# Leaving a streaming kernel with one barrier instead of two, with GpSimd awaiting the last store

## The chip, the cores and the metric

The kernel runs on one core of a Trainium2 chip. The metric is device time in microseconds (us) of one execution, lower being better. Nanoseconds are written ns.

A few words that recur. An engine is one of the core's five units with its own instruction stream: TensorE, VectorE (DVE in the profile), ScalarE (ACT), GpSimd (POOL) and SyncE (SP, which issues the transfers here). They synchronise by semaphores. Drains and events are instructions of an engine's instruction stream that wait for semaphores or add to them; the exit is built of them. The span is the time from the first to the last instruction of the kernel in a trace. The landing is the last update of the last store's semaphore.

## The reference, cut to what matters

```python
def setup_inputs():
    return {"x": np.random.randn(64, 256, 8192).astype(np.float32)}

def reference(x):
    return np.mean(x, axis=2)
```

Half a gigabyte is read, 64 KB are written.

## The kernel before

All loads are issued by SyncE, in 63 blocks of 256 rows and one last block in small pieces. VectorE sums along rows, with a little help from ScalarE. TensorE transposes the sums of the 63 blocks for one store; the last block goes out in two stores of half a kilobyte. The very last store is this:

```python
    def store_last(r):
        nc.vector.transpose(out=fin_t[r][:], in_=fin[r][:])
        return nc.sync.dma_start(out=out_last[r], in_=fin_t[r][0:P:SQ, :])
    ...
    untracked(scaled_sum(fin[1][:, 0:1], fin_in[:, 0 : lastw + k]))._wait_ge(sem, 16)
    with tc.issue_after(st.ins):
        store_last(1)
    ctx.close()
    tc.close()
    tc.compile()
```

What matters here stands in no line of the source: closing the tile context adds an exit block. In the built program it reads as follows (each engine runs its own lines in this order; G is the gather semaphore of the barrier, R its release semaphore):

```
SyncE    3 event waits and a drain: the 3 stores, and the last work of the 4 other engines
ScalarE, TensorE, VectorE, SyncE   drain: when R is 0, add 1 to G
ScalarE, TensorE, VectorE, SyncE   event: when R is 1 or more, take 1 from R
GpSimd   drain; event (gather): when G is 4, take 4 from G; event (release): add 4 to R
GpSimd   drain (reset); clear of the kernel's semaphores 99 to 118
the four engines and GpSimd        a second barrier, the same as the first
```

## Time and profile before

| | before |
|---|---|
| median of the timed runs | 1246.84 us (1246.76 to 1246.90, 3 runs) |
| span of the profiled execution | 1245.24 us |
| last transpose ends | 1242.76 us |
| last store issued | 1242.79 us |
| landing | 1244.35 us |
| landing to end of span | 898 ns |

The times from "last store issued" on are single records of the trace: starts of instructions, and updates of semaphores. No view prints the updates; they were read from the trace file itself, here and below. This is how to read the exit as a view. Each row is one engine, with q for its sequencer (PEldq is TensorE's), and one operation at the line of the exit; then the count, the shortest, middle and longest duration in ns, and the start of the first and the last, in us. Before:

```profile
L172 SPq EVENT_SEMAPHORE  x5: 17/28/28, 1243.4 to 1245.2; - x5
L172 POOLq EVENT_SEMAPHORE  x4: 17/17/17, 1244.5 to 1245.1; - x4
L172 POOLq DRAIN  x3: 34/89/389, 1.1 to 1245.0; - x3
L172 SPq DRAIN  x3: 7/7/13, 1244.4 to 1244.7; - x3
...
L172 PEldq EVENT_SEMAPHORE  x2: 51/51/51, 1244.7 to 1245.2; - x2
```

SyncE has five events (three waits, two releases) and GpSimd four (two gathers, two releases). TensorE's event, the longest at 51 ns, is there twice: once for each barrier. The second ends the span.

### The profile page before, as it was taken

What the parts mean: (1) busy time and instruction counts of PE and PEld (TensorE: products, weight loads), DVE (VectorE), ACT (ScalarE), POOL (GpSimd) and SP (SyncE); (2) the same over time, 40 slices, a digit from 0 to 9 for tenths busy, and PEclk for the clock granted to TensorE, in tenths of its full rate; (3) what the DMA queues carried; (4) which work ended last, traced back from release to release, by engine and by line L of the source; (5) the groups of instructions that cost most, each with busy time, mean ns of one, the idle gap of its engine ahead of it and who ended that gap; (6) DMA issues with size and microseconds to landing.
All of it is one profiled execution on the core that took longest, in us unless ns stands there. A gap on an engine that the chain in (4) does not pass through costs nothing.

```text
span 1245.2 us, 227 instructions
## 1 busy us (share of the span) xinstructions
PE 0.9 (0%) x2; PEld 0.4 (0%) x2; DVE 1087.4 (87%) x79; ACT 16.5 (1%) x13; POOL 0.7 (0%) x6
## 2 busy tenths in 40 slices
PE   0000000000000000000000000000000000000000
PEld 0000000000000000000000000000000000000000
DVE  3898988989889889898898988989889898898898
ACT  0000000000000000000000000000000000000004
POOL 0000000000000000000000000000000000000000
DMA  9999999999999999999999999999999999999998
GB/s 438 417 425 438 438 438 438 434 408 438 438 438 438 438 438 432 411 438 438 438 438 438 438 415 427 438 438 438 438 438 436 406 438 438 438 438 438 438 429 348
DMA packets 10169, 536.95 MB, mean 431 GB/s; under 512 B 1145, under 2 KB 1464, under 8 KB 1720
## 3 DMA queue, kind: packets, MB, share of 16 engines
q1 hardware_dynamic: 10168, 536.94, 99.8%
q14 instruction: 1, 0.01, 0.0%
HBM read 536.87 MB, written 0.07 MB: 431 GB/s over the span
## 4 chain that ended last, share of the span: by engine, by line
DMA 70%; DVE 29%; SPq 0%; issue 0%; DVEq 0%
DMA xt<-in_x_dram 70%; DVE res L92 29%; DVE fin_in L92 0%; SPq L82 0%; DVE fin_in L98 0%; DVE fin_t L109 0%; DVEq L98 0%
## 5 line engine op out<-in xcount | busy, mean ns | idle before, releaser
L92 DVE TENSOR_REDUCE res<-xt 128x2 f32<-128x16384 f32 (+1 forms) x63 | 1076.4, 17086 | 153.3 <-DMA xt<-in_x_dram 153.3
L95 ACT ACT_TABLE_LOAD x1 | 1.3, 1283 | 1181.3 <-DVE res L92 1181.3
L95 ACT ACTIVATE xt<-xt 128x8192 f32<-128x8192 f32 (+5 forms) x6 | 14.7, 2443 | 43.9 <-DMA xt<-in_x_dram 43.7
L92 DVE TENSOR_REDUCE fin_in<-xt 128x1 f32<-128x256 f32 (+3 forms) x5 | 5.0, 1005 | 0.3 <-DMA xt<-in_x_dram 0.2
L92 DVE TENSOR_REDUCE head<-xt 128x1 f32<-128x4096 f32 x1 | 4.4, 4420 | 0.2 <-DMA xt<-in_x_dram 0.2
L153 PE MATMUL ps<-ident,res 128*63 128x128 f32 x2 | 0.9, 460 | 1230.4 <-ACT xt L95 1229.3
L95 ACT ACTIVATION_READ_ACCUMULATOR xt<-xt 128x1 f32 x6 | 1.1, 186 | 0.0
L72 DVE MEMSET fin<- 128x32 f32 x2 | 0.1, 85 | 0.9 <-PEq L230 0.9
L154 DVE TENSOR_SCALAR bulk<-ps 63x128 f32<-63x128 f32 x2 | 0.6, 278 | 0.4 <-PE ps L153 0.4
L153 PEld LDWEIGHTS ps<-ident,res 128*63 128x63 f32 x2 | 0.4, 180 | 1230.6 <-issue 1229.2
L98 DVE TENSOR_SCALAR_CACHE_REDUCE fin_in<-fin_in 128x265 f32<-128x265 f32 x1 | 0.4, 431 | 0.2 <-DVE fin_in L92 0.2
L109 DVE STREAM_TRANSPOSE fin_t<-fin 128x32 f32<-128x32 f32 x2 | 0.4, 212 | 0.1
L60 POOL TENSOR_SCALAR_AFFINE_SELECT ident<-ident 128x128 f32<-128x128 f32 x1 | 0.3, 295 | 0.1
L98 DVE TENSOR_SCALAR_CACHE_REDUCE head<-head 128x2 f32<-128x2 f32 x1 | 0.2, 156 | 0.1
L59 POOL MEMSET ident<- 128x128 f32 x1 | 0.2, 205 | 0.4 <-POOLq L230 0.4
L230 POOL MEMSET const-bfloat16-1.0<- 128x1 bf16 x1 | 0.1, 103 | 0.0
L230 POOL MEMSET const-uint8-127<- 128x1 uint8 x1 | 0.1, 103 | 0.0
L230 POOL MEMSET const-float32-0.0<- 128x1 f32 x1 | 0.1, 99 | 0.2 <-issue 0.2
L230 POOL MEMSET const-float32-1.0<- 128x1 f32 x1 | 0.1, 99 | 0.0
L98 DVE DVE_READ_ACCUMULATOR head<-head 128x1 f32 x1 | 0.1, 85 | 0.0
L98 DVE DVE_READ_ACCUMULATOR fin_in<-fin_in 128x1 f32 x1 | 0.1, 84 | 0.0
## 6 DMA issues: line engine op xcount, KB each, us to landing
xt<-in_x_dram SPq DMA_DIRECT2D x1, 4096.0 KB, 31.2
xt<-in_x_dram SPq DMA_DIRECT2D x1, 2048.0 KB, 35.7
xt<-in_x_dram SPq DMA_DIRECT2D x1, 1024.0 KB, 37.7
xt<-in_x_dram SPq DMA_DIRECT2D x63, 40.8
xt<-in_x_dram SPq DMA_DIRECT2D x1, 512.0 KB, 38.5
xt<-in_x_dram SPq DMA_DIRECT2D x1, 256.0 KB, 38.7
xt<-in_x_dram SPq DMA_DIRECT2D x1, 128.0 KB, 38.6
fin_in<-in_x_dram SPq DMA_DIRECT2D x1, 128.0 KB, 38.4
```

Of the source, the lines that this page charges most:

```text
L59: nc.gpsimd.memset(ident[:], 0.0)
L60: nc.gpsimd.affine_select(out=ident[:], in_=ident[:], compare_op=mybir.AluOpType.not_equal, fill=1.0, base=0, pattern=[[-1, P]], channel_m ...
L72: nc.vector.memset(fin[r][:], 0.0)
L92: return untracked(nc.vector.tensor_reduce(out=dst, in_=src, axis=X, op=ADD))
L95: return untracked(nc.scalar.activation(out=src, in_=src, func=COPY, accum_out=dst))
L98: return nc.vector.tensor_scalar(out=src, in0=src, scalar1=inv, scalar2=None, op0=mybir.AluOpType.mult, op1=ADD, accum_out=dst,)
L109: nc.vector.transpose(out=fin_t[r][:], in_=fin[r][:])
L153: nc.tensor.transpose(out=ps[:LB, :], in_=res[:, r, :], identity=ident[:])
L154: nc.vector.tensor_scalar_mul(out=bulk[:LB, :, r], in0=ps[:LB, :], scalar1=inv)
L230: nc = _bacc.Bacc("TRN2", target_bir_lowering=False, num_devices=1)
```

## The change

The exit keeps one barrier. SyncE no longer awaits the last store. GpSimd's gather does, beside the four arrivals. Then GpSimd clears the semaphores, and only then releases the others. The second barrier, SyncE's own drain and GpSimd's drains around the clear go away.

```diff
-        store_last(1)
+        last_store = store_last(1)
...
+    exit_ins = list(end_bb.instructions)
+    waiter, waits = exit_ins[0], exit_ins[0].sync_info.on_wait
+    stored = last_store.ins.sync_info.on_update[0].id
+    drain, gather, release, _, clear = [
+        i for i in exit_ins if i.engine == mybir.EngineType.Pool
+    ][:5]
+    with nc.body("awaits", parent=parent, valid_engines=[mybir.EngineType.SP]):
+        for w in waits:
+            if w.id != stored:
+                nc.sync.wait_ge(bass.SemaphoreHandle(w.ant_name, w.id), w.wait_value)
+    bass.BassInstruction(gather)._wait_ge(
+        bass.SemaphoreHandle(last_store.ins.sync_info.on_update[0].ant_name, stored), 16
+    )
...
+    end_bb.instructions = [
+        *awaits.instructions, *exit_ins[1 : exit_ins.index(drain)], drain, gather, clear, release
+    ]
```

(Two asserts and the lines that take the helper block out of the list are cut.)

More of the change, by code (lines that the diff above doesn't have):

```diff
@@ L215 @@
     head_bb.instructions.insert(at, hint)
+    exit_ins = list(end_bb.instructions)
+    waiter, waits = exit_ins[0], exit_ins[0].sync_info.on_wait
+    assert waiter.engine == mybir.EngineType.SP and isinstance(waiter, mybir.InstDrain)
+    stored = last_store.ins.sync_info.on_update[0].id
+    drain, gather, release, _, clear = [
+        i for i in exit_ins if i.engine == mybir.EngineType.Pool
+    ][:5]
+    assert isinstance(clear, mybir.InstISA)
+    with nc.body("awaits", parent=parent, valid_engines=[mybir.EngineType.SP]):
[5 more added lines that the diff above has]
+    )
+    awaits = next(b for b in blocks if b.name == "awaits")
+    blocks.remove(awaits)
+    end_bb.instructions = [
+        *awaits.instructions, *exit_ins[1 : exit_ins.index(drain)], drain, gather, clear, release
+    ]
 _INS = ['x']
```

## The prediction

> **What bounds the kernel now.** I read the page from the top, then the chain of work that ended last, then the waits of SyncE, then the instructions of the exit, and at last the single records of the final 3 us. The page's head, its slices and its chain say what the 1245 us are made of:
>
> ```profile
> span 1245.2 us, 227 instructions
> PE 0.9 (0%) x2; PEld 0.4 (0%) x2; DVE 1087.4 (87%) x79; ACT 16.5 (1%) x13; POOL 0.7 (0%) x6
> DMA  9999999999999999999999999999999999999998
> HBM read 536.87 MB, written 0.07 MB: 431 GB/s over the span
> DMA xt<-in_x_dram 70%; DVE res L92 29%; DVE fin_in L92 0%; SPq L82 0%; DVE fin_in L98 0%; DVE fin_t L109 0%; DVEq L98 0%
> ```
>
> The 16 DMA engines are at 90% or more in every slice but the last. The kernel streams 536.87 MB; VectorE, busy for 87%, keeps step behind it. The bound of the whole is the load. Nothing in this change touches a load or a sum, so at most the last few microseconds can move. The chain, in order of time, shows where the work stops:
>
> ```profile
> 1240.44 1.49 DVE fin_in L92 x3
> ...
> 1242.07 0.45 DVE fin_in L98 x2
> 1242.52 0.02 issue
> 1242.55 0.21 DVE fin_t L109
> ```
>
> The last computing instruction, the transpose, ends at 1242.76 us; the span ends at 1245.24. So 2.48 us at the end are store and exit. The waits of SyncE from 1242 to 1246 us (who waited for whom; us in total, times, longest) split them:
>
> ```profile
> SPq L110 <- DVE fin_t L109: 1.2, 1, 1.2
> SPq L172 <- DMA out_dram<-fin_t: 0.9, 1, 0.9
> SPq L172 <- PEq L172: 0.6, 2, 0.5
> ```
>
> The second line is SyncE waiting for the last store to land. The third is its two waits for the release in two barriers; the engine named is only whoever touched the release semaphore, the release itself comes from GpSimd. The instructions on the exit's line from 1244.69 us on (durations in ns) show that barrier number two is nearly empty of work:
>
> ```profile
> L172 POOLq DRAIN  x1: 89/89/89, 1244.7 to 1244.7; - x1
> ...
> L172 POOLq EVENT_SEMAPHORE_RANGE_CLEAR  x1: 142/142/142, 1244.8 to 1244.8; - x1
> ```
>
> **The exit, record by record.** Starts in us, from the trace: last store issued by SyncE 1242.786 (511 ns of issue); the last update of its semaphore 1244.346; SyncE's event wait for it starts 1244.363, its plain drain 1244.428, its barrier drain 1244.498; that one's update arrives 1244.506. GpSimd's gather starts 1244.530, its release 1244.608, update 1244.633. Then GpSimd alone: drain 1244.694, clear of the semaphores 1244.813, drain 1244.983, second gather 1245.062, second release 1245.140, update 1245.165. TensorE leaves last: its event starts 1245.193 and takes 51 ns, to 1245.244, which is the end of the span.
>
> **What the Trainium skill says.** "Perfetto Trace Analysis", section "Sequencer-only Instruction (DRAIN, etc)": the profiler reports only the execution, not the wait before it nor the spread of the semaphore update after it. The trace agrees: GpSimd's gather is recorded with 17 ns, but from its start to the next instruction's start are 78 ns, and its update is seen 25 ns after its start. So I add starts, not durations. "DMA: Bandwidth & Descriptors", section "Anatomy of one DMA — SWDGE (gpsimd) path": of a fixed cost of about 2 us most is the receipt of the write, and the semaphore can't fire before it. Here issue to landing is 1244.346 - 1242.786 = 1.56 us for 0.5 KB, issued by SyncE rather than GpSimd; the same kind, somewhat shorter, and nothing that a barrier can shorten. "Runtime: NRT & Kernel Launch", section "The ~15µs preamble/postamble breakdown": after the kernel the runtime runs its own barrier over all engines. The trace shows it: updates of a semaphore that is not the kernel's run from 1245.523 to 1246.003 and again to 1247.149.
>
> **The change part by part.** It takes away SyncE's wait for the last store with the drain behind it, GpSimd's three drains but the first, the whole second barrier (a drain and an event wait on each of four engines, a gather and a release on GpSimd). It adds one condition to GpSimd's gather: the last store's semaphore at 16. In the built program this is one instruction with two waits and its decrement, not two instructions. It moves the clear between gather and release. The loads, sums and stores are the same on all engines, in the same order.
>
> SyncE's other waits are done well before: its first event wait starts at 1243.368 and successive ones are about 70 ns apart, so with three waits and the barrier drain it arrives near 1243.61, 0.7 us before the store lands. The other three engines have arrived by then: the updates of the gather semaphore by ScalarE and VectorE are at 1241.673 and 1242.818, TensorE's earlier. So the store stays the last thing waited for.
>
> From the landing at 1244.346 to the end, before:
> - landing to the release of barrier one: 1244.633 - 1244.346 = 287 ns;
> - release one to release two: 1245.165 - 1244.633 = 532 ns;
> - release two to TensorE's end: 1245.244 - 1245.165 = 79 ns. Sum 898 ns.
>
> After:
> - landing to GpSimd's gather: 24 ns (as 1244.506 to 1244.530);
> - gather to clear: 78 ns (gather to release before, start to start), or 89 as an event with two waits is recorded with 28 rather than 17 ns on SyncE;
> - clear to release: 170 ns (clear to drain before, start to start); up to 33 more if the pause before an event after the clear is the 61 ns seen between two events and not the 28 ns seen before the drain;
> - release to update 25 ns; update to TensorE's end 79 ns.
> Sum 376 to 420 ns. Removed: 898 - 420 = 478 to 898 - 376 = 522 ns; I take 500.
>
> All of this is on the path, none of it beside other work: after the landing nothing else runs. Span after: 1245.24 - 0.50 = 1244.74 us. The timed runs stand 1246.84 - 1245.24 = 1.60 us above the span (the profiled execution itself read 1247.03). I keep that as a constant, since every engine is let go by the same release event as before: 1244.74 + 1.60 = 1246.34 us, 0.04% less.
>
> **The rivals.**
> (a) The runtime's barrier swallows part. Its first eight updates are 35, 160, 44, 23, 99, 39, 34 and 46 ns apart (differences of the records); at the start of the execution the same walk has 34, 39, 44, 23, 113, 38, 34 and 47. The second step is thus some 120 ns late: one engine comes late to it. If what delays that engine does not hang on the kernel's release, up to 0.12 us of the gain is lost (1246.46), in the worst case all (1246.84). Against it: all engines come from the same release, so their lateness should move along.
> (b) Instruction fetches. The exit gets shorter by 2 to 4 instructions on each engine, so what follows lies elsewhere. "Runtime: NRT & Kernel Launch", section "Instruction fetch mechanics", says that a taken branch out of the present window forces a fetch before execution goes on. The trace has one 8192-byte instruction transfer near the end, at 1242.604, 43 ns after VectorE's branch, of 455 ns; it is over at 1243.06, long before the release, so it is hidden. If a fetch came onto the path it would cost some 0.5 us at least (estimate from that transfer) and eat the gain: 1246.8 to 1247.3. Fewer instructions make an added fetch unlikely.
> (c) A wait takes the place of the one removed: GpSimd wakes more slowly from the store's semaphore than SyncE (17 ns), or the clear right behind a wait costs more than behind a drain. Every such step costs tens of ns: 0.1 us, 1246.45.
> (d) Nothing to be seen: the three runs lie within 0.14 us, but another load of the program may shift 1246 us of streaming by more than 0.5 us; the transfers' slices range from 406 to 438 GB/s. This moves the result both ways.
>
> **Range and chances.** (a) to (c) lean upwards by 0 to 0.5 us, (d) adds about 0.5 us either way. I take 1245.5 to 1247.1. Two per cent are 25 us; the whole stretch after the last computation is 2.5 us, so neither side is in reach: 0.995 for within 2%, the rest for a disturbance of the chip.
>
> **What would show it right or wrong.** Right: in SyncE's waits at the exit the line for the store is gone and the release wait occurs once, about 0.9 us long or more; one clear, GpSimd with two event instructions at the exit instead of four and one drain; landing to end of span near 0.40 us against 0.90; store issue to landing still about 1.56 us; span about 0.5 us less as far as the last transpose ends at the same time. Wrong in a step: clear or release starts more than 50 ns off the sums above (c), an instruction transfer after 1243 us (b), the runtime's updates not closer behind the kernel's end as before (a), or the last transpose moving by more than the gain (d).

## The result

| | before | after |
|---|---|---|
| median of the same rounds | 1246.87 us (1246.76 to 1247.29, 6 runs) | 1246.30 us (1246.10 to 1246.69, 6 runs) |
| mean of the same rounds | 1246.91 us | 1246.37 us |
| span of the profiled execution | 1245.24 us | 1244.90 us |
| landing to end of span | 898 ns | 367 ns |

The ratio is 0.9996, with a 95% interval of 0.9983 to 1.0009: the same, by the 2% measure. A ratio here is the mean time of one kernel's fast runs over that of the other's of the same rounds, so not quite the ratio of the medians. The output is correct.

The page's head and the end of the chain of work, after:

```profile
span 1244.9 us, 214 instructions
...
HBM read 536.87 MB, written 0.07 MB: 431 GB/s over the span
```

```profile
1242.26 0.45 DVE fin_in L98 x2
1242.70 0.02 issue
1242.73 0.21 DVE fin_t L109
```

The stream is as before: the same bytes at the same rate. In this execution the last transpose even started 0.18 us later (1242.73 against 1242.55), which is why the two spans differ by 0.35 us only. From the transpose's end at 1242.94 to the end of the span the kernel takes 1244.90 - 1242.94 = 1.96 us, against 2.48. SyncE's waits near the end, after:

```profile
SPq L110 <- DVE fin_t L109: 1.2, 1, 1.2
SPq L172 <- PEq L172: 0.9, 1, 0.9
```

SyncE's wait for the store is gone. In its place it waits once, 0.9 us, for the only release. The time of the store did not vanish: another engine waits for it. The exit after:

```profile
L172 POOLq EVENT_SEMAPHORE  x2: 17/272/526, 1244.0 to 1244.8; - x2
L172 POOLq DRAIN  x1: 386/386/386, 1.1 to 1.1; - x1
...
L172 SPq DRAIN  x1: 253/253/253, 1243.8 to 1243.8; - x1
L172 POOLq EVENT_SEMAPHORE_RANGE_CLEAR  x1: 139/139/139, 1244.6 to 1244.6; - x1
...
L172 PEldq EVENT_SEMAPHORE  x1: 51/51/51, 1244.8 to 1244.8; - x1
```

GpSimd has two events instead of four. One of them, the gather, is recorded with 526 ns: its record opens when the four arrivals are there (1244.032) and closes after the store has landed (1244.558), so part of the wait shows as duration. TensorE has one event. In single records, counted from the landing, with the end of the last instruction of GpSimd and of the span:

| ns after the landing | before | after |
|---|---|---|
| GpSimd's gather starts / ends | 184 / 201 | before the landing / 30 |
| first release starts | 262 | none |
| clear starts | 467 | 94 |
| last release starts | 794 | 263 |
| GpSimd's last instruction ends | 811 | 280 |
| TensorE's last instruction ends: end of span | 898 | 367 |

So 531 ns went from the exit. The store itself took the same from issue to landing (1.560 and 1.562 us).

### The profile page after: what moved, and what is told of

Same layout as the page of the kernel before. It is cut to its first block, busy times and chain, and to the rows that moved or that the text cites. A ratio compares the mean times of both kernels' runs of the same rounds, so it can differ in the third digit from the quotient of the medians.

```text
span 1244.9 us, 214 instructions
## 1 busy us (share of the span) xinstructions
PE 0.9 (0%) x2; PEld 0.4 (0%) x2; DVE 1087.4 (87%) x79; ACT 16.5 (1%) x13; POOL 0.7 (0%) x6
## 4 chain that ended last, share of the span: by engine, by line
DMA 70%; DVE 29%; SPq 0%; issue 0%; DVEq 0%
DMA xt<-in_x_dram 70%; DVE res L92 29%; DVE fin_in L92 0%; SPq L82 0%; DVE fin_in L98 0%; DVE fin_t L109 0%; DVEq L98 0%
```

## The experiments

The totals of the full kernels scatter by some tenths of a microsecond. So most experiments use a short kernel: cut to 4 of its 64 blocks, it keeps the exit word for word and has a sixteenth of the stream. Such a kernel leaves most of the output unwritten, and its result is wrong. Its edit is one line:

```diff
-    N = B * C
+    N = 4 * 256
```

**The two kernels, cut.**

> The kernel before, cut to the first 4 of the 64 blocks of rows (the rest of the output is not written, so the result is wrong on purpose), so that the streaming and its scatter shrink by 16 while the exit stays word for word. All theories: last landing of the store to end of span 0.90 us as in the long kernel, store issue to landing about 1.56 us. Total near 85 us (536.87 MB take 1240 us, so 33.6 MB take 78, and some 8 for start and end), scatter of the runs below 0.2 us.

> The changed kernel, cut likewise. Main theory (the gain is the exit, all of it on the path): landing to end of span 0.37 us, and the timed total is 0.53 us below short_before. Rival 1 (the 0.57 us between the long medians are partly scatter of the streaming, or the runtime's closing barrier swallows a part): the records of the exit shrink by 0.53 but the total falls by 0.4 or less. Rival 2 (something earlier also became faster): the total falls by more than 0.6.

Measured: 85.59 us in the median before (85.48 to 85.80, 5 runs) and 85.17 after (85.04 to 85.27, 5 runs). The means are 85.61 and 85.15, so 0.46 us apart. From landing to end of span 893 and 368 ns, issue to landing 1.552 and 1.555 us. The exit is the one of the long kernel, to 5 ns in its length. The scatter of the short kernel before is 0.32 us rather than the 0.2 expected, so the scatter does not come from the stream alone. The difference of 0.46 lies between main theory and rival 1, so these totals alone don't decide; the records of the closing walk (the runtime's own barrier after the kernel, below) do.

**Only the wait moved.** Both barriers stay; GpSimd's first gather awaits the store. SyncE's own drain, which held one of its waits, goes away too.

```diff
-    end_bb.instructions = [
-        *awaits.instructions, *exit_ins[1 : exit_ins.index(drain)], drain, gather, clear, release
-    ]
+    end_bb.instructions = [*awaits.instructions, *exit_ins[1:]]
```

> One part alone: GpSimd's first gather awaits the last store, SyncE awaits the rest, both barriers and the drains stay. Main theory: landing to the first release's start falls from 262 to 94 ns (as measured in the changed kernel up to its clear), the rest stays, so 0.73 us from landing to end and 0.17 us less than short_before in total. Rival (nearly all comes from the barrier taken away, the hop over SyncE lies beside other work): less than 0.05 us.

Measured: 85.51 us in the median (85.33 to 85.66), mean 85.48, so 0.13 below the short kernel before. These runs overlap with that kernel's, so the records must decide. Landing to first release 92 ns, landing to end 729 ns: 164 less than the 893. The hop over SyncE lay on the path. The exit's view of this kernel:

```profile
L172 POOLq EVENT_SEMAPHORE  x4: 17/17/514, 82.6 to 83.7; - x4
...
L172 PEldq EVENT_SEMAPHORE  x2: 51/51/51, 83.2 to 83.7; - x2
```

Four GpSimd events and two of TensorE say that both barriers are there; the 514 ns show the gather that holds the store's wait.

**Only one barrier.** SyncE awaits the store as before.

```diff
-    with nc.body("awaits", parent=parent, valid_engines=[mybir.EngineType.SP]):
-    ... (the wait moved to GpSimd)
     end_bb.instructions = [
-        *awaits.instructions, *exit_ins[1 : exit_ins.index(drain)], drain, gather, clear, release
+        *exit_ins[: exit_ins.index(drain)], drain, gather, clear, release
     ]
```

> The other part alone: one barrier with the clear between gather and release, while SyncE awaits the store as before. Main theory: landing to GpSimd's gather 184 ns as before, 78 to the clear, 170 to the release, 104 to the end: 0.54 us, so 0.36 us less than short_before. If the parts add up, this and the moved wait make 0.53 together. Rival as for the moved wait: 0.5 us or more from this part alone.

Measured: 85.26 us (85.10 to 85.38), mean 85.25, so 0.37 below the mean of the short kernel before. Landing to end 532 ns, 361 less. The parts add up: 164 + 361 = 525 ns, and both together measured 893 - 368 = 525. The view shows SyncE awaiting the store, and one barrier:

```profile
SPq L172 <- DMA out_dram<-fin_t: 0.9, 1, 0.9
SPq L172 <- PEq L172: 0.3, 1, 0.3
```

**Where the time goes after the kernel's end.** The timed runs stand about 1.8 us above their spans in both kernels (1246.69 against 1244.9 in the profiled execution after). In the trace, after the kernel's last instruction, one semaphore of the runtime is updated nine times, then again nine times. The first series is taken here as a closing walk that the engines take part in one after the other; the kernels without a release, below, bear this out. In the changed kernel its steps come 606, 640, 852, 896, 919, 1017, 1056, 1090 and 1137 ns after the landing. The third comes 212 ns after the second, where most are 23 to 47 ns apart: some engine is late there. The next experiments ask which, and whether it hides part of the gain.

> The changed kernel once more, at full size, in more rounds. Main theory: 0.51 us below the kernel before (0.53 in the exit, 0.01 given back in the runtime's closing walk). If the 0.57 us between the first medians were partly scatter, the difference of the means lies elsewhere, but between 0.3 and 0.7.

Measured: 1246.18 us in the median (1245.95 to 1246.92, 5 runs) against 1246.69 (1246.50 to 1246.94, 9 runs) for the kernel before on that chip. The means are 1246.29 and 1246.69, 0.40 us apart. From landing to end of span 367 ns again, and the same nine steps to within 1 ns.

**No release at all.** The other engines add to the gather and leave; GpSimd clears and leaves.

```diff
-    end_bb.instructions = [
-        *awaits.instructions, *exit_ins[1 : exit_ins.index(drain)], drain, gather, clear, release
+    leave = [
+        i
+        for i in exit_ins[1 : exit_ins.index(drain)]
+        if not isinstance(i, mybir.InstEventSemaphore)
     ]
+    assert len(leave) == 4
+    end_bb.instructions = [*awaits.instructions, *leave, drain, gather, clear]
```

> The changed kernel, full size, without the release: the other engines add to the gather and leave, GpSimd clears and leaves; the runtime's own closing walk over the engines is then what joins them. The kernel's end is then the end of the clear, 94 + 139 = 233 ns after the landing, against 367: span 0.13 us less. What the total does tells which engine holds up the closing walk. If GpSimd is the engine that comes late to its third step (about 565 ns after GpSimd's last instruction in both kernels), it only starts some 47 ns sooner and the total falls by 0.05 us. If it is one of the engines that wait for the release, the total falls by 0.13 to 0.24 us.

> The same cut to 4 of 64 blocks (wrong result on purpose), beside short_after with 85.15 us in the mean: landing to end of span 0.23 us. Last update of the closing walk counted from the landing: 1.14 us in the changed kernel; 1.08 if GpSimd is the late engine, 0.9 to 1.0 if not.

Measured: at full size 1246.40 us (1245.96 to 1246.76), mean 1246.37, which is not below the 1246.29 of the changed kernel on that chip. Cut, 85.11 us (84.99 to 85.92), mean 85.24 with the one run at 85.92. The span falls as expected, 233 ns from landing to end, but the totals show no gain that stands out of the scatter. The trace tells why. The first step of the walk now comes 12.8 us before the landing, shortly after TensorE's exit, and the second 2.5 us before it, 159 ns after ScalarE's. The third comes 771 ns after the landing, 538 after GpSimd's last instruction, and the walk ends at 1056 instead of 1137 (cut: 770 and 1056). GpSimd is the third step, and its way there is long in itself. The walk gained 81 ns, more than the 47 expected; 37 of them are lost again between the two series, which no run explains. The last update of the second series is at 2238 instead of 2282 ns: 44 ns gained. That is near the 0.05 us expected, in part by luck.

```profile
L172 POOLq EVENT_SEMAPHORE  x1: 519/519/519, 1243.4 to 1243.4; - x1
L172 POOLq EVENT_SEMAPHORE_RANGE_CLEAR  x1: 139/139/139, 1243.9 to 1243.9; - x1
```

These are the last two rows of the exit: no engine has a release event any more, and the clear is the kernel's last instruction.

**Release first, clear last.**

```diff
-        *awaits.instructions, *exit_ins[1 : exit_ins.index(drain)], drain, gather, clear, release
+        *awaits.instructions, *exit_ins[1 : exit_ins.index(drain)], drain, gather, release, clear
```

> The changed kernel, cut likewise, with the release ahead of the clear, so the clear lies beside the others' leaving. The other engines leave 169 ns sooner (release 94 ns after the landing), GpSimd ends about 94 + 78 + 139 = 311 ns after the landing instead of 280. If GpSimd is the engine that the closing walk waits for, the total is the same or 0.03 us more than short_after; if one of the released engines is, it falls by 0.1 us or more.

Measured: 85.21 us (84.96 to 85.26), mean 85.15, the mean of the short changed kernel on another chip. GpSimd's last instruction ends 312 ns after the landing. The other four leave 171 ns sooner, and the first two steps of the walk move with them, from 606 and 640 to 435 and 469. The third does not: 849 against 852. It follows GpSimd alone.

Here is what all traces say together, in ns after the landing:

| kernel | GpSimd's last instruction ends | third step | walk ends | second series ends |
|---|---|---|---|---|
| before, full | 811 | 1372 | 1657 | 2803 |
| short before | 805 | 1366 | 1652 | 2796 |
| short, wait moved only | 640 | 1202 | 1487 | 2630 |
| short, one barrier only | 444 | 1016 | 1301 | 2446 |
| after, full | 280 | 852 | 1137 | 2282 |
| short, clear last | 312 | 849 | 1135 | 2278 |
| no release, full | 233 | 771 | 1056 | 2238 |

The third step comes 537 to 572 ns after GpSimd's last instruction in every row. It is 537 or 538 where the clear is GpSimd's last instruction, and 561 to 572 where a release event is. So the gain that reaches the outside follows GpSimd's own end, within 25 ns in these rows: for the change itself 811 - 280 = 531 became 2803 - 2282 = 521 ns.

**SyncE takes the exit over.** If GpSimd is slow on the way to the walk, it should not be the last to leave. Here there is no barrier of the kernel's own: SyncE awaits by their semaphores the last units of the others and the three stores, then clears. The engines are joined by the runtime's walk alone.

```diff
-    bass.BassInstruction(gather)._wait_ge(
-        bass.SemaphoreHandle(last_store.ins.sync_info.on_update[0].ant_name, stored), 16
-    )
+        nc.sync.wait_ge(
+            bass.SemaphoreHandle(last_store.ins.sync_info.on_update[0].ant_name, stored), 16
+        )
+        nc.sync.sem_clear(range(99, 119))
...
-    end_bb.instructions = [
-        *awaits.instructions, *exit_ins[1 : exit_ins.index(drain)], drain, gather, clear, release
-    ]
+    end_bb.instructions = [*awaits.instructions]
```

> Full size, no barrier of the kernel's own at the end: SyncE awaits the last units of the four other engines and the three stores by their semaphores, the last store last, then clears the range itself; the others leave as soon as their work is done. Only the runtime's closing walk joins them. From the earlier runs GpSimd is the third step of that walk and takes 538 to 572 ns from its last instruction to it, while the step that the released engines answer for comes about 240 to 285 ns after their last instruction. If the 540 ns belong to GpSimd and SyncE is among the quick ones (the fifth, turning step), the first walk ends some 0.7 to 0.8 us after the landing against 1.14 in the changed kernel, and the total falls by 0.3 to 0.4 us below the changed kernel. Rival: the 540 ns belong to whichever engine leaves last; then the walk ends at about 1.05 us and the total falls by 0.1 us or less.

> The changed kernel again at full size, on the same chip as sp_exit, to compare with it: 0.5 us below the kernel before, within a scatter of the means of about 0.15 us; from the landing to the span's end 0.367 us and to the end of the first walk 1.137 us as in its two traces so far.

> The same exit by SyncE in the kernel cut to 4 of 64 blocks (wrong result on purpose), where the scatter of the totals is about 0.1 us: 0.3 to 0.4 us below short_after_again if GpSimd's way to the walk is slow in itself, 0.1 or less if it is the last engine's whoever that is. Landing to end of the kernel's span about 0.23 us either way.

> The changed kernel, cut to 4 of 64 blocks, again, on the chip of short_sp_exit: 85.15 us in the mean as before, give or take 0.1; landing to end of span 0.368 us.

Measured, all on one chip:

| | median | mean |
|---|---|---|
| before, full | 1246.81 us (1246.60 to 1247.14, 9 runs) | 1246.83 |
| after, full | 1246.17 us (1246.11 to 1246.79, 5 runs) | 1246.35 |
| exit by SyncE, full | 1245.59 us (1245.28 to 1245.85, 5 runs) | 1245.58 |
| after, cut | 85.10 us (85.07 to 85.21, 5 runs) | 85.12 |
| exit by SyncE, cut | 84.46 us (84.33 to 84.82, 5 runs) | 84.55 |

The full version is correct in these runs; that its engines may leave one by one rests on the runtime's walk, which joins them. It is 0.77 us below the changed kernel in the mean and 1.25 below the kernel before; cut, 0.57 below the changed kernel. None of its runs overlaps one of the other two. By the 2% measure it is the same too (0.9989, interval 0.9976 to 1.0003). I had expected 0.3 to 0.4 us; two things are cheaper than thought. The exit's two last rows of SyncE, each from the view of its own line, are:

```profile
L232 SPq EVENT_SEMAPHORE  x1: 28/28/28, 1244.3 to 1244.3; - x1
```

```profile
L235 SPq EVENT_SEMAPHORE_RANGE_CLEAR  x1: 61/61/61, 1244.4 to 1244.4; - x1
```

The same clear of 20 semaphores takes 61 ns on SyncE against 139 on GpSimd, so the span ends 142 ns after the landing. And SyncE is in the walk 126 ns later, at 268 ns, as its fifth and turning step; the four others had taken theirs before the landing. The walk ends at 432 ns against 1137, and the second series at 1618 against 2282 (cut: 426 and 1616): 0.66 us by the records, between the 0.57 and 0.77 of the totals. The rival, by which the 540 ns belong to whichever engine leaves last, falls.

## Why the prediction was right

**The bound and the reach.** Right. The stream did not change, nothing but the exit moved, and the result is within 2%. The forecast was 1246.34 us, measured were 1246.30.

**The sum of the exit.** Right in mechanism and nearly in size: 478 to 522 ns were worked out for the removed part, 531 were measured. After the landing 376 to 420 ns were expected, and 367 came. The mis-sized term is the step from landing to clear: 24 ns to the gather and 78 to 89 from there, 102 to 113 in all, against 94 measured. The gather does not start afresh at the landing; it is already open and ends 30 ns after it. Clear to release measured 169 against 170 (the extra 33 for a pause did not come), release to end 104 as worked out.

**What lies beside other work.** The prediction had SyncE at the barrier near 1243.61, 0.7 us before the landing. Its arrival came at 1244.007, in an execution that ran 0.18 us late throughout, so about 0.22 us later than worked out. The reason is the barrier drain: 253 ns in place of the 7 ns that it took behind a landed store. It cost nothing, as the landing came 0.52 us later still. The prediction took the duration of a drain from a place behind a landed store; here it stood behind a store just issued. What the drain waits for is not shown.

**The constant of 1.60 us.** Wrong as a number, harmless in use. It set a timed median against the span of another, slower execution. Where each run's span is listed beside its time, the difference is about 1.8 us in both kernels, and it cancels.

**Rival (a), the closing walk.** The observation was right: one engine is late to the third step. The fear was wrong for this change: the engine is GpSimd, whose lateness is counted from its own last instruction, and that moved by the full 531 ns. The walk swallowed 10 ns. The prediction's counter-argument, that all engines come from the same release, fits the other four only: GpSimd gives the release and does not wait for it. With the clear last, the four left 171 ns sooner and the third step stayed. The worked example for a swallowed gain is the kernel without release: its span fell by 134 ns and the records to the end by 44.

**Rival (b), fetches.** No instruction transfer after 1243 us in the trace after; the one of 8192 bytes comes 51 ns after the start of VectorE's branch, as before (43 ns). **Rival (c)** fell: every step measured at or below its estimate. **Rival (d)** was right as a caution: three comparisons of the full kernels gave 0.54, 0.40 and 0.49 us in the means, and the spans of single executions lie up to 0.9 us apart for one and the same kernel (1244.2 to 1245.1 in the second round of the changed kernel). The slices that it gives as 406 to 438 GB/s leave out the last one, of 348.

What stays open: why SyncE's drain lasts until 1.041 to 1.050 us after the issue of the store in front of it (nine traces), and what GpSimd does in its 540 to 570 ns. The traces show no instruction there. Nor was a kernel without its own clear tried. In every trace at least 18 of the 20 semaphores that it clears (99 to 118) are updated once more between the two series, within 0.34 us after the first. Whether that makes the kernel's own clear needless, with the 169 ns from its start to the release, is not shown.

## What to carry to other kernels

The last landing starts a chain of semaphore hops which nothing hides. Here it was 0.90 us long. Count the hops from there, start to start. Letting the engine that clears await the store itself was worth 0.16 us here, and leaving out the second barrier 0.36 us; together that is 0.04% of the long kernel and 0.6% of the short one. Judge by what comes after the kernel's own last instruction as well, since a shorter span need not be a shorter execution. The engine that leaves last should be one that is quickly in the runtime's closing walk: SyncE here, not GpSimd.

## What the Trainium skill lacked or had wrong

- "Perfetto Trace Analysis", section "Sequencer-only Instruction (DRAIN, etc)": it has the profiled duration begin when all semaphores are satisfied. GpSimd's gather with two waits is recorded from 24 ns after the arrivals were complete until 30 ns after the landing, 508 to 526 ns in the full kernels: with two waits, the second one is inside the recorded duration. SyncE's events with two waits, the second satisfied already, show 27 or 28 ns.
- "Runtime: NRT & Kernel Launch", section "The ~15µs preamble/postamble breakdown": it gives the closing barrier as a wait for all engines, without saying that the engine which leaves last matters. Here the order of the walk is TensorE, ScalarE, GpSimd, VectorE, SyncE and back, and its start depends on the engine: 537 to 572 ns from GpSimd's last instruction to its step, 126 from SyncE's.
- No page has the cost of the instruction that clears a range of semaphores: 20 of them took 139 to 142 ns on GpSimd and 61 ns on SyncE.
- "VectorE: DVE Perf Modes", section "The DRAIN you can't avoid", gives about 12 ns on all engines for the drains that the runtime puts around a kernel. No page has the drains of a kernel's own exit. In the second barrier they took 7 to 14 ns on four engines; GpSimd's two around the clear took 89 and 34. In the first they took 425 to 528 ns on TensorE and 536 or 537 on ScalarE, open while the engine's last instruction still ran, 10 on VectorE, and on SyncE 252 to 263 where the drain stood right behind a store's issue.
